# Twelve of 22 feature tiles of each FFN's last projection by a seven-product block scheme, with the accumulators corrected in place in PSUM

## The chip, the cores and the metric

The kernel runs on one core of a Trainium2 chip. The metric is the device time of one execution in microseconds (us); lower is better. A difference of under 0.2%, about 2.2 us here, cannot be told from no change.

## The reference

One layer of an encoder on 512 tokens of width 1024, all in float32: a half-step SwiGLU feed-forward network (FFN), two attention branches that are merged by gates, and a second FFN. The change touches the last matrix product of `_swiglu`, in both FFNs:

```python
D_MODEL, SEQ, D_FF = 1024, 512, 2816

def _swiglu(x, w_gate, w_up, w_down):
    return (jax.nn.silu(x @ w_gate) * (x @ w_up)) @ w_down
...
f = _swiglu(_rmsnorm(x, ffn1_pre_g[l]), ffn1_w_gate[l], ffn1_w_up[l], ffn1_w_down[l])
x = x + 0.5 * _rmsnorm(f, ffn1_post_g[l])
```

With 128 features to a tile, `@ w_down` multiplies 512 tokens by 22 feature tiles by 1024 columns.

## The kernel before

Every float32 product is made of three TensorE matmuls on fp32r halves (`mm3`): high by high, high by low, low by high. `split` makes the halves: ScalarE (ACT) casts the value to the high half, VectorE (DVE) subtracts to get the low half. Weights come in pieces of 128 x 1024 numbers (512 KB): `convert` loads one on SyncE's (SP's) DMA queue into a buffer of tag `raw` (two buffers) and splits it into two buffers of tag `w` (twelve buffers, so six split pieces at a time). Other SBUF tiles of 128 x 512 come from a pool of 54 units; PSUM has eight banks of 128 x 512.

An FFN runs in stages. The normed input is `hn_hi`, `hn_lo`, feature-major (8 feature tiles by 512 tokens). Gate and up products of the first three output tiles are plain (`first_pairs`, `pair`). For the other 19 tile pairs `seven` already uses a block scheme with seven products of 12 matmuls of width 256 instead of eight; sums of weight blocks come from accumulating DMAs on GpSimd's (POOL's) queue (`load_blocks`) and from DVE (`sums_of`). `use` and `use7` apply SiLU and leave each hidden tile in `hidden[j]`.

`token_major` is the last projection (and, with eight tiles, the output projection of the mixing stage). Tokens are stationary, weights move, 512 columns at a time. It sums the left 512 columns of all four token tiles over the 22 feature tiles (`acc0`, four banks), then the right 512 columns over the first 14 (`acc1`), then, token tile by token tile, over the last eight, so that the post-norm of one token tile runs beside the matmuls of the next. Each hidden tile is split once (`stat`). In all 22 x 4 x 2 = 176 `mm3`, 528 matmuls of width 512, in each FFN. While the last tile pairs of `seven` are under way, `behind` already converts pieces for `token_major`.

The order on each engine is made when the program is built, by a list scheduler with priorities in the order of the code; in the stretches of `ordered` (the end of an FFN and the start of the next stage) PE, ACT and DVE keep the order of the code, and SP does through the whole first FFN. Each engine and each DMA queue then runs its list in order.

Of the kernel before, what the change touches and what calls it, by code (L numbers as in the profile page):

```python
# [12 lines left out]
F32 = mybir.dt.float32  # L13
# [3 lines left out]
ALU = mybir.AluOpType  # L17
# [23 lines left out]
def block_kernel(ctx, tc, x, gains, weights, rpb_near, rpb_all, alibi0, alibi12, out):  # L41
    nc = tc.nc

    const = ctx.enter_context(tc.tile_pool(name="const", bufs=1))
    big = ctx.enter_context(tc.tile_pool(name="big", bufs=1))
    wp = ctx.enter_context(tc.tile_pool(name="wp", bufs=2 * NPIECE))
    gp = ctx.enter_context(tc.tile_pool(name="gp", bufs=2))
    up = ctx.enter_context(tc.tile_pool(name="up", bufs=NUNIT))
    sp = ctx.enter_context(tc.tile_pool(name="sp", bufs=4))
    pp = ctx.enter_context(tc.tile_pool(name="pp", bufs=8, space=PSUM))  # L50
    dp = ctx.enter_context(tc.tile_pool(name="dp", bufs=1, space=DRAM))
# [11 lines left out]
    def bank(name="ps"):  # L63
        return pp.tile([P, 512], F32, tag="ps", name=name)

    hn_hi = big.tile([P, NK, T], F32R, name="hn_hi")
    hn_lo = big.tile([P, NK, T], F32R, name="hn_lo")
    ident = const.tile([P, P], F32, name="ident")
    mhalf = const.tile([P, 1], F32, name="mhalf")

# [17 lines left out]

    pieces = {}
    loads = deque()  # L90
    state = {"next": 0, "take": 0, "stop": 2 * STD, "ahead": lambda: None}
    ordered = []
    total = weights.shape[0]

# [130 lines left out]
        late.append(lambda: [turned(t, b, xs[b]) for b in range(2)])  # L225

    def turned(t, b, xs):
        pt = bank()
        for i in range(4):
            nc.tensor.transpose(pt[:, i * P:(i + 1) * P], xs[:, i * P:(i + 1) * P], ident)  # L230
# [62 lines left out]
        split(w[:, :512], w[:, 512:], raw)  # L293
        return w

    def seven(use, mv, n_pairs, n0, behind, raws):

        blocks = {}
        o = {}

        def get(j):
            if j < n_pairs and j not in raws:
                raws[j] = load_blocks(n0 + 2 * j)

        def ready(j, i):
            if j < n_pairs:  # L310
                if j and loads:
                    loads.popleft()()
                if i == 1:
                    sums_of(raws[j])
                blocks[j, i] = split_block(raws[j].pop(i))
            elif behind:
                behind()
# [12 lines left out]
        get(0)  # L330
        get(1)
        for i in (1, 5, 2, 6, 3, 7, 4):
            ready(0, i)
        for j in range(n_pairs + 1):
            now, was = j < n_pairs, j > 0
            get(j + 2)
            if now:
                q = product(j, 1, "q", True)
                g, u = res[j] = unit(name="g"), unit(name="up")
                nc.scalar.copy(g[:, :256], q)  # L340
            ready(j + 1, 1)
            if was:
                q0 = product(j - 1, 7, "q", False)
                g0, u0 = res.pop(j - 1)
                nc.vector.tensor_tensor(u0[:, 256:], u0[:, 256:], q0, op=ALU.subtract)
# [12 lines left out]
            ready(j + 1, 3)  # L358
            if was:
                product(j - 1, 4, "q", False)  # L360
                use(j - 1, g0, u0, q0)
            ready(j + 1, 7)
            if now:
                product(j, 3, "p", False)
                nc.vector.tensor_tensor(u[:, :256], p, u[:, :256], op=ALU.subtract)
            ready(j + 1, 4)

    def token_major(n_k, stat, g_post, f, g_pre, store, src=None):

        wt = {}
        first = max(n_k - 8, 0)
        early = [] if store else [n for n in sorted(spread) if n >= state["next"]][:SPREAD]

        def one(acc, t, k, i, start, stop):
            hh, hl = stat(k)
            if t == 0 and i < n_k:
                stat(min(k + 2, n_k - 1))  # L380
            if i // 2 not in wt:
                wt[i // 2] = take(k < first)
            s = slice(t * P, (t + 1) * P)
            mm3(acc, hh[:, s], hl[:, s], *cut(wt[i // 2], (i % 2) * 512, 512), start, stop)

        acc0 = [bank() for _ in range(NT)]
        for k in range(n_k):
            if first == 0 and k % 2 and early:
                convert(early.pop(0))
            for t in range(NT):  # L390
                one(acc0[t], t, k, k, k == 0, k == n_k - 1)
        ss = [small("ssf", 2) for _ in range(NT)]
        for t in range(NT):
            sumsq(acc0[t], ss[t][:, 0:1], f)
        acc1 = [bank() for _ in range(NT)]
        for k in range(first):
            if k > 2 and k % 2 == 0 and early:
                convert(early.pop(0))
            for t in range(NT):
                one(acc1[t], t, k, n_k + k, k == 0, False)  # L400
        fg0 = []
        for t in range(NT):
            u = unit()
# [5 lines left out]
        fill(NPIECE)  # L409
        ordered.append([mark()])  # L410
        for t in range(NT):
            for k in range(first, n_k):
                one(acc1[t], t, k, n_k + k, k == 0, k == n_k - 1)
                if t and not store and k == first + TURN:
                    if t > 1:
                        late.popleft()()
                    pre_norm(t - 1, g_pre, ssx)
# [24 lines left out]

    def ffn(g, store, src):
        hidden = [None] * NF
        parts = {}
        n0 = state["take"]

        def stat(k):
            if k not in parts:
                parts[k] = unit(F32R), unit(F32R)  # L450
                split(*parts[k], hidden[k])
                hidden[k] = None
            return parts[k]

        def use(j, pg, pu):
            h = unit(name="h")
            nc.scalar.activation(h, pg, AF.Silu)
            nc.vector.tensor_tensor(h, pu, h, op=ALU.mult)
            hidden[j] = h

        def use7(j, g, u, q):
            nc.scalar.activation(g[:, :256], g[:, :256], AF.Silu)
            nc.scalar.activation(g[:, 256:], q, AF.Silu)
            nc.vector.tensor_tensor(g, u, g, op=ALU.mult)
            hidden[STD + j] = g
# [20 lines left out]
        def behind():  # L486
            state["next"] = max(state["next"], after)
            state["take"] = after
            fetch()
# [289 lines left out]
    def mixing(g):  # L779
# [168 lines left out]
        token_major(8, lambda k: merged[k], g_post, 1.0, g_pre, False)  # L948


    whole[:] = [[unit(name="whole") for _ in range(2)] for _ in range(2)]
# [167 lines left out]
    return w.reshape(-1, 2, P, w.shape[1] // 512, 512).transpose(3, 0, 2, 1, 4).reshape(-1, P, PIECE)  # L1119


# [43 lines left out]
```

## Time and profile before

| | us |
|---|---|
| median of 3 runs | 1121.98 (1121.58 to 1122.52) |
| the profiled execution | 1121.61 |
| span of its profile | 1119.8 |
| PE busy in the span | 1111.2 (99%) |
| DVE busy | 726.7 (65%) |
| ACT busy | 587.0 (52%) |
| POOL busy | 99.5 (9%) |

The profile shows one execution. PE is TensorE's matmuls and PEld its loads of the stationary operand, which overlap the matmuls. A matmul's time in the profile is from its start to its modelled end, and neighbours overlap, so the rate of PE is read from the starts of consecutive matmuls. The 1.8 us between the span and the profiled execution's time lie outside the profiled instructions.

### The profile page before, as it was taken

What the parts mean: (1) busy time and instruction counts of PE and PEld (TensorE: products, weight loads), DVE (VectorE), ACT (ScalarE), POOL (GpSimd) and SP (SyncE); (2) the same over time, 40 slices, a digit from 0 to 9 for tenths busy, and PEclk for the clock granted to TensorE, in tenths of its full rate; (3) what the DMA queues carried; (4) which work ended last, traced back from release to release, by engine and by line L of the source; (5) the groups of instructions that cost most, each with busy time, mean ns of one, the idle gap of its engine ahead of it and who ended that gap; (6) DMA issues with size and microseconds to landing.
All of it is one profiled execution on the core that took longest, in us unless ns stands there. A gap on an engine that the chain in (4) does not pass through costs nothing.

```text
span 1119.8 us, 18253 instructions
## 1 busy us (share of the span) xinstructions
PE 1111.2 (99%) x6959; PEld 1004.4 (90%) x6959; DVE 726.7 (65%) x1336; ACT 587.0 (52%) x1188; POOL 99.5 (9%) x156
## 2 busy tenths in 40 slices
PE   9999999999999999999999999999999999999997
PEld 7999999998888988888988888889999999998886
DVE  6887777783245678886467645657877777782313
ACT  6555555572233667767656643245555555571210
POOL 3112111000002000000000000013111111000001
PEclk9999999999999999999999999999999999999999
DMA  5889998443362353422232323356577776543412
GB/s 207 218 185 254 230 234 201 108 119 108 94 192 90 109 166 121 132 76 81 72 100 76 85 85 95 95 170 174 127 182 189 162 185 187 123 133 104 169 48 75
DMA packets 77576, 155.71 MB, mean 139 GB/s; under 512 B 22065, under 2 KB 24625, under 8 KB 77490
## 3 DMA queue, kind: packets, MB, share of 16 engines
q1 hardware_dynamic: 63856, 134.17, 37.8%
q0 software_dynamic: 10944, 19.93, 11.5%
q8 instruction: 54, 0.88, 0.3%
q10 hardware_dynamic: 2690, 0.46, 0.2%
q14 instruction: 32, 0.26, 0.1%
HBM read 149.50 MB, written 7.58 MB: 140 GB/s over the span
## 4 chain that ended last, share of the span: by engine, by line
PE 99%; DVE 0%; POOL 0%; issue 0%; ACT 0%; DVEq 0%; POOLq 0%; ACTq 0%
PE ps L154 20%; PE ps L156 20%; PE ps L155 20%; PE q L154 7%; PE q L155 7%; PE q L156 7%; PE p L155 3%; PE p L154 3%; PE p L156 3%; PE r L154 2%; PE r L155 2%; PE r L156 2%; PE ps L692 1%; PE ps L719 1%; PE ps L230 1%; PE ps L661 1%
## 5 line engine op out<-in xcount | busy, mean ns | idle before, releaser
L86 DVE TENSOR_TENSOR w<-raw,w 128x1024 fp32r<-128x1024 f32 (+1 forms) x200 | 194.7, 978 | 210.0 <-ACT w L85 200.3
L85 ACT CAST w<-raw 128x1024 fp32r<-128x1024 f32 (+1 forms) x200 | 169.7, 854 | 237.1 <-PE ps L155 149.9
L154 PE MATMUL ps<-hn_hi,w 128*128 128x512 f32 (+1 forms) x512 | 181.9, 355 | 0.0
L156 PE MATMUL ps<-hn_hi,w 128*128 128x512 f32 (+1 forms) x512 | 179.4, 350 | 0.0
L155 PE MATMUL ps<-hn_lo,w 128*128 128x512 f32 (+1 forms) x512 | 179.3, 350 | 0.0
L154 PE MATMUL ps<-w,u 128*128 128x512 f32 (+1 forms) x456 | 177.2, 389 | 0.0
L155 PE MATMUL ps<-w,u 128*128 128x512 f32 (+1 forms) x456 | 176.8, 388 | 0.0
L156 PE MATMUL ps<-w,u 128*128 128x512 f32 (+1 forms) x456 | 176.8, 388 | 0.0
L86 DVE TENSOR_TENSOR w<-t,w 128x512 fp32r<-128x512 f32 x152 | 104.1, 687 | 32.1 <-ACT w L85 32.1
L85 ACT CAST w<-t 128x512 fp32r<-128x512 f32 x152 | 93.7, 619 | 41.9 <-ACT w L85 17.8
L156 PEld LDWEIGHTS ps<-hn_hi,w 128*128 128x128 f32 x512 | 96.9, 189 | 12.8
L155 PEld LDWEIGHTS ps<-hn_lo,w 128*128 128x128 f32 x512 | 97.0, 190 | 11.5
L154 PEld LDWEIGHTS ps<-hn_hi,w 128*128 128x128 f32 x512 | 97.0, 189 | 11.5
L156 PEld LDWEIGHTS ps<-w,u 128*128 128x128 f32 x456 | 85.7, 188 | 17.5
L154 PEld LDWEIGHTS ps<-w,u 128*128 128x128 f32 x456 | 85.7, 188 | 17.1
L155 PEld LDWEIGHTS ps<-w,u 128*128 128x128 f32 x456 | 85.7, 188 | 16.9
L154 PE MATMUL q<-hn_hi,w 128*128 128x256 f32 x304 | 86.2, 284 | 0.0
L155 PE MATMUL p<-v,w 128*128 128x256 f32 x304 | 86.1, 283 | 0.0
L155 PE MATMUL q<-hn_lo,w 128*128 128x256 f32 x304 | 86.1, 283 | 0.0
L155 PE MATMUL q<-v,w 128*128 128x256 f32 x304 | 86.1, 283 | 0.0
L156 PE MATMUL q<-v,w 128*128 128x256 f32 x304 | 86.1, 283 | 0.0
L156 PE MATMUL q<-hn_hi,w 128*128 128x256 f32 x304 | 86.1, 283 | 0.0
(163 smaller groups left out, 2302.1 us busy)
## 6 DMA issues: line engine op xcount, KB each, us to landing
raw<-in_weights_dram SPq DMA_DIRECT2D x156, 512.0 KB
t<-in_weights_dram SPq DMA_DIRECT2D x76, 256.0 KB
t<-in_weights_dram POOLq DMA_DIRECT2D x76, 256.0 KB, 5.3
w<-in_weights_dram SPq DMA_DIRECT2D x38, 256.0 KB
x<-in_x_dram SPq DMA_DIRECT2D x16, 256.0 KB
table<-bias_d SPq DMA_DIRECT2D x12, 256.0 KB
gain<-in_gains_dram SPq DMA_DIRECT2D x5, 512.0 KB
table<-in_alibi_dram SPq DMA_DIRECT2D x8, 256.0 KB
```

The lines of the kernel that those rows point to most:

```text
L85: nc.scalar.copy(hi, src)
L86: nc.vector.tensor_tensor(lo, src, hi.bitcast(F32), op=ALU.subtract)
L154: nc.tensor.matmul(o, sh, mh, start=start, stop=False, **kw)
L155: nc.tensor.matmul(o, sh, ml, start=False, stop=False, **kw)
L156: nc.tensor.matmul(o, sl, mh, start=False, stop=stop, **kw)
L230: nc.tensor.transpose(pt[:, i * P:(i + 1) * P], xs[:, i * P:(i + 1) * P], ident)
L661: nc.tensor.matmul(ps[:, o:o + w], q[:, cols], windows(wide, kl, i), start=False, stop=True)
L692: nc.tensor.transpose(ps[:, i * P:(i + 1) * P], s, ident)
L719: nc.tensor.matmul(o, vv[n][:, h], m, start=first, stop=(n == 3 and part == 1), skip_group_check=True)
```

## The change

Twelve of the 22 feature tiles are taken out of the plain sum. They form three block products: each takes two blocks of two feature tiles, two halves of 256 tokens and two halves of 512 columns, and makes seven products of two feature tiles x 256 tokens x 512 columns (12 matmuls each) instead of eight. With BLOCKS = 6 pairs of feature tiles there are 3 x 7 = 21 products per FFN, in the order of `seq`, where `(i, d)` is product i of block product d and `("o", n)` a part of the ten tiles that stay plain. So 12 tiles x 4 x 2 = 96 `mm3` become 84.

The output stands in eight banks: `r` and `c` are the left and right columns of the first 256 tokens, `q` and `z` those of the other 256. Products run into `r`, `q` or `c`; at four places in `seq` (`after`) one accumulator is added to or taken from another by `onto`: ACT copies the two banks to SBUF, DVE adds them to the two others in place, and later matmuls go on summing there.

The token sums are made on DVE (`tokens`) from the hidden tiles, which `times` now writes by half-tokens into `duos`. The weight sums are made by accumulating DMAs of 512 KB on POOL's queue (`t1`, `t3`, `t4`) and by DVE (`t2 = t1 + W11`, under `rows`). Every product needs its own split of a 128 x 512 token tile and of a 128 x 1024 weight tile; `prep` does it six places ahead in `seq` (AHEAD), the first six under the last two rounds of `seven` (`lead`). The 32 KB per partition of `hn_hi`, `hn_lo` become four tiles of a pool `hp`, which the weight sums (`ta`, `tb`, `ba`, `bb`) take over when `seven` has read a half for the last time; `renew` gives them back. The pieces of `w_down` are reordered on the host (`_down_pieces`).

```diff
+BLOCKS = 6
+AHEAD = 6
+ORDER = [*range(STD, STD + 2 * BLOCKS), *range(STD), *range(STD + 2 * BLOCKS, NF)]
-    big = ctx.enter_context(tc.tile_pool(name="big", bufs=1))
+    hp = ctx.enter_context(tc.tile_pool(name="hp", bufs=4))
...
-        seven(use7, next(sums), NF - STD, n0 + 2 * STD, behind, raws)
-        token_major(NF, stat, g_post, 4.0, g_pre, store, src)
+        far, lead, rest = down(after, duos, stat, g_post, g_pre, store, src)
+        state["next"] = state["take"] = after + 2 * BLOCKS
+        seven(use7, next(sums), NF - STD, n0 + 2 * STD, lambda q: [f() for f in q.popleft()], far, lead, raws)
+        rest()
...
+            if kind == "t1":
+                raw[key] = duo_room(*at)
+                nc.sync.dma_start(raw[key], block(0, 0, d))
+                nc.gpsimd.dma_start(raw[key], block(0, 1, d), accum_op=add)
+                return
...
+            if kind == "t3":
+                nc.sync.dma_start(raw[key], block(0, 1, d))
+                nc.gpsimd.dma_start(raw[key], block(1, 1, d), accum_op=add)
...
+        def fourth(d):
+            raw["t4", d] = raw.pop(("t2", d))
+            nc.gpsimd.dma_start(raw["t4", d], block(1, 0, d), accum_op=add)
...
+            x, y, op = {5: (hc, hd, sub), 6: (v[d], ha, sub), 3: (v[d], hb, add)}[i]
+            nc.vector.tensor_tensor(v[d], x, y, op=op)
...
+            if i == 6:
+                t = raw["t2", d] = raw.pop(("t1", d))
+                nc.vector.tensor_tensor(t, t, raw[(1, 1), d], op=add)
+                return t
...
+                split_tokens(s, tokens(*s))
+                split_rows(s, rows(*s))
+        into = {1: "q", 2: "r", 3: "c", 4: "q", 5: "c", 6: "q", 7: "q"}
...
+        def onto(x, y, op):
+            for t in range(2):
+                u = unit(name="part")
+                with tc.high_priority(offset=URGENT):
+                    nc.scalar.copy(u, acc[y][t])
+                nc.vector.tensor_tensor(acc[x][t], acc[x][t], u, op=op)
+        after = {(1, 2): ("r", "q", add), (5, 2): ("z", "c", add), (6, 2): ("c", "q", sub), (7, 2): ("z", "q", sub)}
+        seq = [(2, 0), (2, 1), (1, 0), (1, 1), (1, 2), ("o", 1), (5, 0), (5, 1), (5, 2), (6, 0), ("o", 2),
+               (6, 1), (6, 2), (2, 2), (7, 0), (7, 1), (7, 2), (3, 0), ("o", 3), (3, 1), ("o", 4), (3, 2),
+               ("o", 5), (4, 0), ("o", 6), (4, 1), ("o", 7), (4, 2)]
+        far = deque([[ld(((1, 0), 0), "u"), ld(((1, 0), 1), "u")], [ld(((0, 0), 0)), ld(((0, 0), 1))], []])
+        lead = deque([
+            [ld(("t1", 0), "ta", 0)], [pr(0)], [ld(("t1", 1), "ta", 1)], [pr(1)], [ld(((0, 0), 2))],
+            [pr(2)], [ld(("t1", 2), "tb", 0)], [pr(3)], [], [pr(4)], [], [pr(5)], [], []])
...
```

What it moves on the engines is seen best where the first FFN passes from `seven` to the last projection. DVE before, behind its last correction of a gate/up tile: it splits hidden tiles (`g` to `u`) and pieces (`raw` to `w`).

```order
L86 TENSOR_TENSOR u_3511<-g_1803,u_3510 128x512
L86 TENSOR_TENSOR w_3262<-raw_3259,w_3261 128x1024
L86 TENSOR_TENSOR u_3527<-g_1943,u_3526 128x512
L86 TENSOR_TENSOR u_3543<-g_2083,u_3542 128x512
L86 TENSOR_TENSOR u_3559<-g_2223,u_3558 128x512
```

DVE now, somewhat later, at the splits of products (6, 0) and (6, 1): L610 makes `t2`, L604 token sums, L672 the correction in PSUM, L111 the splits.

```order
L610 TENSOR_TENSOR ta_3198<-ta_3198,ba_3390 128x1024
L111 TENSOR_TENSOR a_3459<-v_3380,a_3458 128x512
L610 TENSOR_TENSOR ta_3198<-ta_3198,ba_3390 128x1024
L604 TENSOR_TENSOR v_3431<-v_3431,h_1488 128x512
L610 TENSOR_TENSOR tb_3315<-tb_3315,bb_3417 128x1024
L672 TENSOR_TENSOR r_3393<-r_3393,part_3495 128x512
L604 TENSOR_TENSOR v_3380<-v_3380,h_1772 128x512
L111 TENSOR_TENSOR w_3464<-ta_3198,w_3463 128x1024
L672 TENSOR_TENSOR r_3394<-r_3394,part_3498 128x512
L111 TENSOR_TENSOR a_3503<-v_3407,a_3502 128x512
L111 TENSOR_TENSOR w_3508<-ta_3198,w_3507 128x1024
```

The split of the weights of (6, 0) now stands behind three sums that need the loads into `ba` and `bb`, and behind a correction that needs product (1, 2).

POOL before, at the end of the first FFN's `seven`: the two accumulating loads of a tile pair (L281, L282), then nothing until the norm.

```order
L281 DMA t1_2757<-in_weights_dram 128x512
L282 DMA t3_2758<-in_weights_dram 128x512
L281 DMA t1_2890<-in_weights_dram 128x512
L282 DMA t3_2891<-in_weights_dram 128x512
L212 TENSOR_SCALAR ms0_4046<-ssf_3710 128x1
```

POOL now: nine accumulating loads of twice the size, for `t1` (L558), `t3` (L568) and `t4` (L574).

```order
L309 DMA t1_2916<-in_weights_dram 128x512
L310 DMA t3_2917<-in_weights_dram 128x512
L558 DMA ta_3198<-in_weights_dram 128x1024 x2
L558 DMA tb_3315<-in_weights_dram 128x1024
L568 DMA tb_3315<-in_weights_dram 128x1024
L568 DMA bb_3417<-in_weights_dram 128x1024
L568 DMA raw_3535<-in_weights_dram 128x1024
L574 DMA ta_3198<-in_weights_dram 128x1024 x2
L574 DMA tb_3315<-in_weights_dram 128x1024
L237 TENSOR_SCALAR ms0_4172<-ssf_3376 128x1
```

A stretch in which POOL's queue was empty now carries nine loads whose data the products wait for.

ACT before, near the end of `seven`: splits alone (and a SiLU, L463).

```order
L463 ACTIVATE g_3157<-q_3144 128x256
L85 CAST u_3606<-g_2643 128x512
L85 CAST u_3622<-g_2778 128x512
L85 CAST u_3638<-g_2911 128x512
L85 CAST u_3654<-g_3034 128x512
L85 CAST w_3286<-raw_3284 128x1024
```

ACT now, where it copies `c` out of PSUM (L671) before the plain part ("o", 2) may go on summing there:

```order
L110 CAST w_3531<-tb_3315 128x1024
L110 CAST w_3556<-raw_3467 128x1024
L110 CAST a_3574<-v_3572 128x512
L110 CAST w_3578<-tb_3315 128x1024
L671 COPY part_3594<-c_3538 128x512
L671 COPY part_3597<-c_3539 128x512
```

The copies stand behind the cast `w_3578`, which reads `t3` of block product 0 and so waits for the fourth accumulating load.

More of the change, by code (lines that the diff above doesn't have):

```diff
@@ L90, in block_kernel @@
     loads = deque()
-    state = {"next": 0, "take": 0, "stop": 2 * STD, "ahead": lambda: None}
+    state = {"used": False, "next": 0, "take": 0, "stop": 2 * STD, "ahead": lambda: None}
     ordered = []
@@ L294, in split_block, with seven @@
         return w
-    def seven(use, mv, n_pairs, n0, behind, raws):
+    def seven(use, mv, n_pairs, n0, behind, far, lead, raws):
         blocks = {}
@@ L307, in get @@
                 raws[j] = load_blocks(n0 + 2 * j)
+            elif j >= n_pairs:
+                behind(far)
         def ready(j, i):
@@ L315, in ready @@
                 blocks[j, i] = split_block(raws[j].pop(i))
-            elif behind:
-                behind()
+            else:
+                behind(lead)
         def product(j, i, key, start):
@@ L411, in token_major @@
         for t in range(NT):
-            for k in range(first, n_k):
-                one(acc1[t], t, k, n_k + k, k == 0, k == n_k - 1)
-                if t and not store and k == first + TURN:
+            for k in ks:
+                one(t, k)
+                if t and not store and k == ks[TURN]:
                     if t > 1:
@@ L444, in ffn, with times @@
         hidden = [None] * NF
+        duos = [[None] * BLOCKS for _ in range(2)]
         parts = {}
         n0 = state["take"]
+        def times(j, a, b):
+            k = ORDER.index(j)
+            if k >= 2 * BLOCKS:
+                hidden[k] = b
+                nc.vector.tensor_tensor(b, a, b, op=ALU.mult)
+                return
+            for i in range(2):
+                if k % 2 == 0:
+                    duos[i][k // 2] = unit(name="h")
+                to = duos[i][k // 2][:, (k % 2) * 256:(k % 2) * 256 + 256]
+                part = slice(i * 256, i * 256 + 256)
+                nc.vector.tensor_tensor(to, a[:, part], b[:, part], op=ALU.mult)
         def stat(k):
@@ L457, in use @@
             nc.scalar.activation(h, pg, AF.Silu)
[L458 to L459 removed]
+            times(j, pu, h)
         def use7(j, g, u, q):
```

203 lines of the change are left out of this document (175 added, 28 removed).

## The prediction

> **What bounds the kernel now.** I read the busy times first, then the chain that ended last, then what PE waited for, and last the last projection of the first FFN by itself. The first fence has one line of the page's busy times and one of its chain, by engine:
>
> ```profile
> PE 1111.2 (99%) x6959; PEld 1004.4 (90%) x6959; DVE 726.7 (65%) x1336; ACT 587.0 (52%) x1188; POOL 99.5 (9%) x156
> PE 99%; DVE 0%; POOL 0%; issue 0%; ACT 0%; DVEq 0%; POOLq 0%; ACTq 0%
> ```
>
> PE fills the span, and the chain that ends last is PE for 99%. All the waits of PE in the trace are two:
>
> ```profile
> PE warm L987 <- DVE idle L955: 1.2, 1, 1.2
> PE ps L230 <- DVE u L1005: 0.6, 1, 0.6
> ```
>
> They come to 1.8 us, at the start. So PE has no stall to lose around the change: each matmul taken out shortens the run by its interval, and each new stall lengthens it by its whole length. The windows by stage (us, then busy time and count of PE, PEld, DVE, ACT, POOL, then granted clock, DMA share, GB/s): `seven`, the last projection of the first FFN, and that of the second:
>
> ```profile
> 128.00:246.00 118.00, 118.00 (x957) 116.75 (x956) 90.53 (x151) 72.81 (x144) 15.91 (x18) 1.00 0.68 176
> 255.00:345.00 90.00, 90.00 (x399) 74.56 (x398) 27.77 (x30) 24.51 (x34) 0.49 (x2) 1.00 0.45 142
> 1010.00:1100.00 90.00, 90.00 (x398) 74.56 (x397) 21.83 (x21) 17.52 (x24) 2.15 (x6) 1.00 0.30 96
> ```
>
> In the last projection DVE is busy for 28 of 90 us and ACT for 25; the spare time there is what the change uses. In `seven`, where the first products are prepared, DVE is already busy for 91 of 118 us.
>
> **What is taken out.** The last projection's matmuls run evenly; of 31 in a row, the first and the last:
>
> ```profile
> 255.00 0.39 PE L156 MATMUL ps<-w,u 128*128 128x512 f32 x1
> 261.80 0.39 PE L156 MATMUL ps<-w,u 128*128 128x512 f32 x1
> ```
>
> 30 intervals in 6.80 us are 0.2267 us each. Per FFN 96 `mm3` become 84, so 36 matmuls go: 8.16 us, and 16.3 us for both. What runs after PE's last matmul stays. The profiled execution took 1121.61 us (span 1119.8 and 1.8 around it), so 1105.3; its time lies 0.4 us under the median of the runs, 1121.98, and from the median the sum is **1105.7 us**. That holds if DVE, ACT and the loads keep ahead.
>
> **What is added on DVE and ACT.** Times by start to next start, from the end of `seven` in the first FFN:
>
> ```profile
> 239.10 0.42 DVE L365 TENSOR_TENSOR up<-p,up 128x256 f32<-128x256 f32 x1
> 239.43 0.68 DVE L464 TENSOR_TENSOR g<-up,g 128x512 f32<-128x512 f32 x1
> 240.03 1.89 DVE L86 TENSOR_TENSOR u<-g,u 128x512 fp32r<-128x512 f32 x3
> 241.84 0.41 DVE L345 TENSOR_TENSOR up<-up,q 128x256 f32<-128x256 f32 x1
> 242.17 3.10 DVE L86 TENSOR_TENSOR u<-g,u 128x512 fp32r<-128x512 f32 x5
> 245.18 1.22 DVE L86 TENSOR_TENSOR w<-raw,w 128x1024 fp32r<-128x1024 f32 x1
> 246.31 1.29 DVE L86 TENSOR_TENSOR u<-g,u 128x512 fp32r<-128x512 f32 x2
> L404 DVE TENSOR_TENSOR u<-ps,gain 128x512 f32<-128x512 f32 x12 | 7.7, 683 | 2.2 <-ACT junk L204 2.1
> L594 ACT COPY vt<-ps 128x512 f32<-128x512 f32 x4 | 2.3, 580 | 0.0
> ```
>
> A 512-wide operation takes 0.60 us (five in 3.01), a 1024-wide one 1.13, a 256-wide one 0.33. Of the last two rows, from the groups, one reads PSUM on DVE at 683 ns, the duration of a read from SBUF, so `onto` gets 0.60; the other is a copy on ACT, 0.58. Per FFN: 21 products split 0.60 + 1.13 = 36.3 us; 12 token sums 7.2; three `t2` 3.4; eight corrections 4.8; together 51.7, in place of twelve hidden tiles and twelve pieces at 20.8. That is 31 us more on DVE, over 110 us in which it had about 75 us free: no cost by its sum. ACT gets nine more splits at 1.67 and eight copies at 0.58, some 20 us in as much room. `times` now writes halves: 12 x (2 x 0.33 - 0.60) = 0.7 us more DVE in `seven`, covered by its 27 us of idle time. What can cost is only order: whether one split is late for its product.
>
> DVE's order from the product of the last gate/up tile (239.43): up to the split of (5, 2) stand four 1024-wide, nine 512-wide and one 256-wide operation, 10.3 us, to 249.7. That split's weight buffers come free when PE has finished product (1, 1). PE's rows give when:
>
> ```profile
> 237.32 0.40 PE L154 MATMUL ps<-w,u 128*128 128x512 f32 x1
> ...
> 238.70 0.28 PE L154 MATMUL q<-v,w 128*128 128x256 f32 x1
> 238.82 0.28 PE L155 MATMUL q<-v,w 128*128 128x256 f32 x1
> ...
> 240.14 0.40 PE L154 MATMUL ps<-w,u 128*128 128x512 f32 x1
> L85 ACT CAST w<-raw 128x1024 fp32r<-128x1024 f32 x108 | 113.5, 1053 | 196.6 <-PE ps L155 149.6 <-DMA raw<-in_weights_dram 32.7 <-issue 5.3
> ```
>
> PE's order has six matmuls, the last but one product of `seven` (12 at 0.12), 26 matmuls (to 246.03), the last product of `seven` (to 247.47), and 16 matmuls: (1, 1) ends at 251.1. ACT's cast takes 1.05, so DVE subtracts at 252.2. From there to the end of the split of (6, 0) are five 1024-wide and five 512-wide operations, 8.7 us: 260.9. PE reaches (6, 0) after 76 matmuls, 247.47 + 17.2 = 264.7. **The slack is 3.8 us** for (6, 0), 4.2 for (6, 1), 3.9 for (6, 2). This is the tightest place I found, and it is why I cost DVE at nothing; by durations in place of intervals 2.9 us are left. If the cover is gone, each us late is a us of the run, and the copies of `c` on ACT are late next.
>
> **What is added on the queues.** Loads grow from 22 to 31 of 512 KB per FFN, nine of them accumulating on POOL's queue. The page's two large queues, the accumulating loads now, their two groups on POOL, one window's answer for tile `t`, and a plain load of 512 KB from its issue to the cast that waited for it:
>
> ```profile
> q1 hardware_dynamic: 63856, 134.17, 37.8%
> q0 software_dynamic: 10944, 19.93, 11.5%
> t<-in_weights_dram POOLq DMA_DIRECT2D x76, 256.0 KB, 5.3
> L282 POOL DMA_DIRECT2D t<-in_weights_dram x38 | 39.5, 1038 | 5.4 <-DMA t<-in_weights_dram 2.0 <-DMA raw<-in_weights_dram 1.2 <-DVE neg L754 0.8
> L281 POOL DMA_DIRECT2D t<-in_weights_dram x38 | 33.2, 874 | 298.3 <-DMA t<-in_weights_dram 108.0 <-DVE w L86 77.2 <-DVE up L345 36.5
> DMA to landing us min/median/max: 3.9/6.3/8.0
> 230.19 0.33 SPq L99 DMA_DIRECT2D raw<-in_weights_dram  x1
> 233.88 1.05 ACT L85 CAST w<-raw 128x1024 fp32r<-128x1024 f32 x1 [0.56 <-DMA raw<-in_weights_dram]
> ```
>
> By volume: q0 took 11.5% of 1119.8 us for 76 loads, 1.7 us each with all sixteen engines, so 3.4 for 512 KB; q1 1.65 for 512 KB. Per FFN nine by 3.4 and no plain load saved (22 remain), 31 us of transfers more against a share of 0.45 in the stage (half of 110 us idle): hidden as a sum. As a latency no row shows an accumulating load of 512 KB. The nearest: two of 256 KB, issued one behind the other, landed by 8.0 us at most; the far end is twice the median in series, 10.6 each. I take 8.0 for the first and 3.4 for each next, since loads sharing engines is what the median of 5.3 for a share of 1.7 looks like, and keep 10.6 in series for the range. POOL's own issue, 0.9 to 1.0 us, has nothing else queued behind it in that stretch.
>
> The first accumulator `t1`(0) needs half of `hn`, read last 72 matmuls of 0.12 before 237.32, so at 228.7; its plain load lands 3.7 us later, 232.4, and POOL issues by 233.4. The load for `t1`(2) lands near 237.5. All three are in by 248.3, where ACT wants `t1`(2) at 251.1. `ba` and `bb` wait for the last product of `seven`, 247.47, and land at 251.1, 252.8 and 254.4; DVE's three sums `t2` stand at 253.9, 255.7 and 257.4. So 2.8 us are spare on each side of the one guess that I could not measure.
>
> SP: loads into `ba`, `bb` wait there for PE until 247.47, and the plain `raw` loads queue behind them; the pieces already converted cover it, since PE needs none of those behind until (2, 2), over 30 us on.
>
> **Rivals.** *Accumulating loads in series (slower).* At 10.6 us each from 233.4, `t1`(2) lands at 265.2, the split of (5, 2) ends at 267.5 in place of 253.3; of the 14.2 late the slack takes 3.8, and 10.4 us per FFN are lost: 1105.7 + 20.8 = 1126.5. It decides from 8.2 us lost per FFN, `t1`(2) landing at about 263, or 9.9 us each. Against it stands the 8.0 for two; for it, that a doubled load may take twice the median, and that POOL's row L281 shows 108 us of waiting for loads of its tile, which are not in the chain only because nothing on PE hung on them.
>
> A stall on PE may cost more than its length. The granted clock after PE's last matmul:
>
> ```profile
> 1112.70 0.39 PE L156 MATMUL ps<-w,u 128*128 128x512 f32 x1
> 1114.00:1116.00 2.00, 0.00 (x0) 0.00 (x0) 1.65 (x4) 0.00 (x0) 0.83 (x2) 1.00 0.00 0
> 1116.00:1118.00 2.00, 0.00 (x0) 0.00 (x0) 0.62 (x2) 0.00 (x0) 0.00 (x0) 0.78 0.78 262
> 1118.00:1119.80 1.80, 0.00 (x0) 0.00 (x0) 0.00 (x0) 0.00 (x0) 0.00 (x0) 0.50 0.00 0
> ```
>
> It stays full for some 4 us and then halves; a stall that long would add to the loss, one of 3 us would not. The Trainium skill, "TensorE: Matmul & The Clock Gate", Part 1 (the HAM clock gate), says that an idle window of about 3.4 us halves the clock until a busy one of about 3.4 us has passed; the trace agrees with the first half. By that rule a stall of 10 us costs an estimated 1.7 us more (3.4 us at half speed), and the series case ends at 1129.9 rather than 1126.5.
>
> *A split late on ACT (gain partly given back).* ACT's copies of `c` out of PSUM stand behind the cast of `w_3578`, which needs `t3`(0), and PE's plain part ("o", 2) may go on in `c` only after them, at 247.47 + 102 matmuls = 270.6. The plain load of `t3`(0) is the next on SP behind `bb` (254.4) and lands at 256.1; its accumulation, issued in 1.0, is in 8.0 later at 265.1, the cast ends at 266.2 and two copies at 267.3: 3.3 us to spare. As the fourth in series (265.2 + 10.6) it would be in at 275.8, the copies would end at 278.0 and each FFN would lose 7.4; half way it is 3.7 each, 7.4 together: **1113.1**. For it: a dozen such in-order meetings, each with only 3 to 4 us to spare. Against: DVE and ACT each have half the stage free to catch up.
>
> *PEld sets the rate.* Then a matmul taken out saves one weight load instead of an interval. In the stage's window 398 loads keep PEld busy for 74.56 us, 0.187 each: 72 x 0.187 = 13.5, and 1108.5. Against it: PEld is 15 of 90 us idle there, while intervals are even. The Trainium skill, "Perfetto Trace Analysis", Identifying the Most-Contended Engine, would judge distance from the limit by weight-load time rather than matmul busy time; here that gives 83% for the stage and does not overturn the even 0.2267.
>
> **How the numbers follow.** The forecast holds at 0.67 (1105.7), a late split 0.18 (1107 to 1118), PEld 0.05, loads in series 0.10 (0.07 slower, 0.03 within what counts as no change: under 0.2%, 2.2 us, nothing can be told). So faster 0.90, same 0.03, slower 0.07. Range: from 1104.3 (the forecast less some 1.4, one and a half times the spread of the three runs) to 1113.1, the middle of the late split; what lies above, some 0.09 of that case and the 0.10, is 0.19.
>
> **What the next profile would show.** Right: 6887 matmuls; PE's waits still about 1.8 us, all at the start; a span near 1103.5; DVE in the first FFN's last projection up from 28 of 90 us to 55 or more. Wrong step by step: PE waiting for ACT at the products (5, 2) to (6, 2) means late loads of `t1`; at ("o", 2), the copies behind `w_3578`; at (6, 0) with DVE as releaser, my ledger; accumulating loads (L558, L568, L574) that take over 9.9 us each, the series. A rate of matmuls other than 0.2267 in the new products would fell the saving itself.

## The result, and the profile after

The changed kernel took 1108.49 us (median of 4 runs, 1108.15 to 1108.89) against 1121.96 us before on the same chip (4 runs, 1121.58 to 1122.52): ratio 0.988, 95% interval 0.9863 to 0.9897. It is faster by 13.5 us where 16.3 were forecast; the time lies in the range, 2.8 us above the forecast. The profiled execution took 1108.66 us with a span of 1106.9. Its busy times and chain:

```profile
PE 1096.3 (99%) x6887; PEld 991.1 (90%) x6887; DVE 791.0 (71%) x1446; ACT 621.7 (56%) x1244; POOL 115.8 (10%) x174
PE 97%; DVE 2%; ACT 0%; issue 0%; POOL 0%; DVEq 0%; POOLq 0%; ACTq 0%
```

The 72 matmuls are gone, and DVE has 2% of the chain that it did not have before. So the first question is whether the matmuls that went were worth their price. The last projection of the second FFN answers it; its first matmul before, and its first and last after (its last before, 1112.70, stands in the prediction):

```profile
990.29 0.40 PE L154 MATMUL ps<-w,u 128*128 128x512 f32 x1
...
984.05 0.40 PE L179 MATMUL r<-w,a 128*128 128x512 f32 x1
1098.29 0.39 PE L181 MATMUL z<-w,u 128*128 128x512 f32 x1
```

From first to last it took 122.41 us and now takes 114.24: 8.17 us less, 36 intervals of 0.227. The saving is there in full. By 984.05 the changed kernel was ahead by 6.24 us, not 8.16: the first FFN lost 1.9. And behind the last matmul the span before went on for 7.1 us (1112.70 to 1119.8), now for 8.6 (1098.29 to 1106.9): 1.5 us more. These three account for it:

| where | us lost |
|---|---|
| first FFN, PE at the end of product (2, 2) | 1.09 |
| first FFN, transposes for the next stage | 0.85 |
| end of the program, behind PE's last matmul | 1.47 |

Their sum is 3.4; 16.3 - 3.4 = 12.9 is the difference of the two spans, 1119.8 - 1106.9. (The medians give 13.5; the first 20 us of a run, before the first FFN's products, differ by up to 1.6 us between the profiled executions of this case.)

Most of the effects below are smaller than the 2.2 us that two times can tell apart, and beside the experiments the kernel before took 1121.52 to 1121.58 us, not 1121.96. So they are read from PE's rows; the times only bear them out. One execution of the first experiment, the profiled one, took 3861.31 us where the other three took 1108.42 to 1109.08, and it is left out.

**The first loss.** All waits of PE in the trace, then PE's, ACT's and DVE's rows around the second of them:

```profile
PE warm L1219 <- DVE idle L1187: 1.2, 1, 1.2
PE r L179 <- ACT w L110: 0.8, 1, 0.8
PE ps L258 <- DVE u L249: 0.4, 1, 0.4
```

```profile
278.08 0.39 PE L181 MATMUL r<-w,a 128*128 128x512 f32 x1
279.26 0.73 PE L179 MATMUL r<-w,u 128*128 128x512 f32 x2 [0.79 <-ACT w L110]
279.83 0.41 PE L179 MATMUL q<-w,a 128*128 128x512 f32 x1
```

```profile
277.12 1.14 ACT L110 CAST a<-v 128x512 fp32r<-128x512 f32 x2 [2.15 <-DVE v L599]
278.17 1.04 ACT L110 CAST w<-raw 128x1024 fp32r<-128x1024 f32 x1
279.11 1.06 ACT L671 COPY part<-q 128x512 f32<-128x512 f32 x2
```

PE waits for the cast of the piece of ("o", 3): the scheduler has put that part's first two matmuls ahead of (7, 0). Behind them (7, 0) goes on in `q`, which ACT must have copied out before (L671). ACT runs its list in order, and cast and copies stand behind a token split (277.12) that waited 2.15 us for a sum of DVE's. The cast has a second late input, the piece itself:

```profile
269.98 1.23 DVE L111 TENSOR_TENSOR w<-raw,w 128x1024 fp32r<-128x1024 f32 x1
271.24 0.33 SPq L124 DMA_DIRECT2D raw<-in_weights_dram  x1
```

Its load was issued at 271.24, when DVE had emptied a `raw` buffer, and the trace has its last packet landing at 277.99, 0.3 us before ACT was through with the token splits. So DVE is late, for both. It has no gap in this stretch; the windows of after, and under the dots the same stretches before:

```profile
232.00:249.00 17.00, 17.00 (x109) 15.45 (x108) 10.98 (x17) 9.14 (x16) 2.62 (x3) 1.00 0.89 212
249.00:258.00 9.00, 9.00 (x42) 7.44 (x41) 9.00 (x13) 4.24 (x8) 0.87 (x1) 1.00 0.97 387
258.00:290.00 32.00, 31.21 (x138) 25.45 (x137) 32.00 (x42) 23.61 (x35) 4.36 (x5) 1.00 0.70 154
255.00:345.00 90.00, 89.22 (x398) 73.56 (x397) 66.14 (x83) 48.17 (x75) 9.49 (x15) 1.00 0.59 167
...
232.00:249.00 17.00, 17.00 (x109) 15.46 (x108) 16.24 (x25) 15.27 (x29) 0.00 (x0) 1.00 0.44 138
258.00:290.00 32.00, 32.00 (x143) 26.52 (x142) 7.00 (x6) 6.07 (x6) 0.00 (x0) 1.00 0.33 99
```

Over the whole stage DVE is busy for 66 of 90 us, but from 249 to 290 us for all of it: it is working off a backlog. And ahead of that, from 232 to 249, it is busy for only 11 of 17 us, while the DMA engines are at 0.89. There it waited (SP's issue, ACT, DVE):

```profile
235.91 0.33 SPq L124 DMA_DIRECT2D raw<-in_weights_dram  x1
...
246.12 1.05 ACT L110 CAST w<-raw 128x1024 fp32r<-128x1024 f32 x1 [7.36 <-DMA raw<-in_weights_dram]
...
240.88 0.42 DVE L375 TENSOR_TENSOR up<-up,q 128x256 f32<-128x256 f32 x1
247.20 1.23 DVE L111 TENSOR_TENSOR w<-raw,w 128x1024 fp32r<-128x1024 f32 x1 [5.90 <-ACT w L110]
```

The piece of ("o", 1) was issued at 235.91 and cast at 246.12, 10.2 us later, where the same load before took 3.7. It shared the engines with two more plain loads and the accumulating loads of `t1`.

The second FFN of the same execution is a control. Its DMA engines are as full at that point, and around the copies PE and ACT have the same order; but DVE has other work ahead of the piece of ("o", 1), and its longest wait there is 1.62 us:

```profile
978.77:995.77 17.00, 17.00 (x109) 15.45 (x108) 14.70 (x22) 10.97 (x20) 3.45 (x4) 1.00 1.02 274
989.11 1.22 DVE L111 TENSOR_TENSOR w<-raw,w 128x1024 fp32r<-128x1024 f32 x1 [1.62 <-ACT w L110]
1022.77 1.05 ACT L110 CAST w<-raw 128x1024 fp32r<-128x1024 f32 x1 [0.57 <-DMA raw<-in_weights_dram]
1023.73 1.06 ACT L671 COPY part<-q 128x512 f32<-128x512 f32 x2
1025.53 0.39 PE L179 MATMUL q<-w,a 128*128 128x512 f32 x1
```

Counted from the first matmul of each last projection (237.28 and 984.05), the copies begin after 41.8 us in the first FFN and after 39.7 in the second, and PE without a stall goes on in `q` after 41.5. In the second FFN it loses nothing. So full engines alone do not make the loss; what differs is how late DVE is.

**The second loss.** Where the first FFN ends, POOL before, and under the dots POOL, DVE and PE after:

```profile
350.11 0.63 POOL L215 TENSOR_SCALAR ms<-ssf,ms 128x1 f32<-128x1 f32 x1 [0.98 <-ACT junk L204]
...
343.01 1.69 POOL L240 TENSOR_SCALAR ms<-ssf,ms 128x1 f32<-128x1 f32 x1 [0.98 <-ACT junk L229]
343.40 1.22 DVE L111 TENSOR_TENSOR w<-raw,w 128x1024 fp32r<-128x1024 f32 x1
350.22 1.32 PE L258 MATMUL ps<-ident,u 128*128 128x128 f32 x8 [0.40 <-DVE u L249]
```

A weight split for the next stage stands on DVE between the norm steps of the first and second token tile; before, it stood ahead of both. POOL's step there took 1.69 us, and 0.63 at its place before, so the norm, and with it PE's transposes, came late. (DVE's own next steps stand behind the split as well; when they were done, DVE waited only 0.17 us more for POOL.) The Trainium skill, "SBUF — State Buffer" (SBUF: two separate sides), says that a DVE operation with two inputs from SBUF and a POOL operation that reads SBUF exclude each other for a whole instruction; the trace agrees, in that POOL's step ends with the 1024-wide subtraction (344.70 and 344.62).

### The profile page after: what moved, and what is told of

It reads as the page before. It is cut to its first block, busy times and chain, and to the rows that moved or that the text cites. A ratio compares the mean times of both kernels' runs of the same rounds, so it can differ in the third digit from the quotient of the medians.

```text
span 1106.9 us, 18356 instructions
## 1 busy us (share of the span) xinstructions
PE 1096.3 (99%) x6887; PEld 991.1 (90%) x6887; DVE 791.0 (71%) x1446; ACT 621.7 (56%) x1244; POOL 115.8 (10%) x174
## 4 chain that ended last, share of the span: by engine, by line
PE 97%; DVE 2%; ACT 0%; issue 0%; POOL 0%; DVEq 0%; POOLq 0%; ACTq 0%
PE ps L179 13%; PE ps L180 13%; PE ps L181 13%; PE q L181 9%; PE q L179 9%; PE q L180 9%; PE p L181 3%; PE p L180 3%; PE p L179 3%; PE r L179 3%; PE r L180 3%; PE r L181 3%; PE c L181 2%; PE c L179 2%; PE c L180 2%; PE ps L924 1%
## 5 line engine op out<-in xcount | busy, mean ns | idle before, releaser
L111 DVE TENSOR_TENSOR w<-raw,w 128x1024 fp32r<-128x1024 f32 (+1 forms) x186 | 177.8, 961 | 135.0 <-ACT w L110 132.7
L110 ACT CAST w<-raw 128x1024 fp32r<-128x1024 f32 (+1 forms) x186 | 155.0, 839 | 167.1 <-PE ps L180 59.7
L179 PE MATMUL ps<-hn,w 128*128 128x512 f32 (+1 forms) x512 | 181.8, 355 | 0.0
L180 PE MATMUL ps<-hn,w 128*128 128x512 f32 (+1 forms) x512 | 179.2, 350 | 0.0
L181 PE MATMUL ps<-hn,w 128*128 128x512 f32 (+1 forms) x512 | 179.1, 350 | 0.0
L111 DVE TENSOR_TENSOR w<-t,w 128x512 fp32r<-128x512 f32 x152 | 104.3, 689 | 31.3 <-ACT w L110 29.6
L181 PEld LDWEIGHTS ps<-hn,w 128*128 128x128 f32 x512 | 96.9, 189 | 12.9
L180 PEld LDWEIGHTS ps<-hn,w 128*128 128x128 f32 x512 | 97.0, 189 | 11.6 <-DVE hn L262 0.2
L179 PEld LDWEIGHTS ps<-hn,w 128*128 128x128 f32 x512 | 97.0, 189 | 11.5
L181 PE MATMUL q<-hn,w 128*128 128x256 f32 x304 | 86.0, 283 | 0.0
L179 PE MATMUL p<-v,w 128*128 128x256 f32 x304 | 86.0, 283 | 0.0
L180 PE MATMUL p<-v,w 128*128 128x256 f32 x304 | 86.0, 283 | 0.0
L180 PE MATMUL q<-v,w 128*128 128x256 f32 x304 | 86.0, 283 | 0.0
L181 PE MATMUL q<-v,w 128*128 128x256 f32 x304 | 86.0, 283 | 0.0
L180 PE MATMUL q<-hn,w 128*128 128x256 f32 x304 | 86.0, 283 | 0.0
L179 PE MATMUL q<-v,w 128*128 128x256 f32 x304 | 86.0, 283 | 0.0
L179 PE MATMUL q<-hn,w 128*128 128x256 f32 x304 | 86.0, 283 | 0.0
L181 PE MATMUL p<-v,w 128*128 128x256 f32 x304 | 85.9, 283 | 0.0
L309 POOL DMA_DIRECT2D t<-in_weights_dram x38 | 33.2, 874 | 296.1 <-DVE w L111 118.5
L179 PEld LDWEIGHTS q<-hn,w 128*128 128x128 f32 x304 | 58.4, 192 | 0.2
L180 PEld LDWEIGHTS q<-hn,w 128*128 128x128 f32 x304 | 58.4, 192 | 0.2
```

Of the source, the lines that this page charges most:

```text
L110: nc.scalar.copy(hi, src)
L111: nc.vector.tensor_tensor(lo, src, hi.bitcast(F32), op=ALU.subtract)
L179: nc.tensor.matmul(o, sh, mh, start=start, stop=False, **kw)
L180: nc.tensor.matmul(o, sh, ml, start=False, stop=False, **kw)
L181: nc.tensor.matmul(o, sl, mh, start=False, stop=stop, **kw)
L309: nc.gpsimd.dma_start(t1, weights[n][:, :512], accum_op=ALU.add)
```

## The experiments

**Each order wrinkle undone by itself.** First, ("o", 3) put back behind (7, 2); nothing else moves:

```diff
+for i in pe[s] if s == ("o", 3) else ():
+    tc.add_manual_dep(i, pe[7, 2][-1].name, ...)
```

> The changed kernel with one thing undone: the first two matmuls of the plain part ("o", 3), which the scheduler had put ahead of the products (7, 0) to (7, 2) of the first FFN, stand behind them; no other engine's order changes. Theory (those two alone were too early for a piece whose split came late): the wait of PE for ACT's cast (0.8 us, 1.05 us of lost intervals) goes and comes back nowhere, PE's last matmul comes 1.05 us earlier, time about 1107.4 us. Rival (DVE's backlog is what counts, and the next product would wait in its place): the stall moves to a product behind, time within 0.3 us of 1108.5.

It took 1109.07 us (1108.42 to 1109.08): no gain. The run with both edits, below, shows PE's row.

Second, one piece less converted ahead at the end of the first FFN:

```diff
-        fill(NPIECE)
+        fill(NPIECE if src is None or store else NPIECE - 1)
```

> The changed kernel with one piece less converted ahead at the end of the first FFN, so that one 128x1024 split (1.13 us on DVE) no longer stands between the steps of the post-norm of the first and the second token tile; PE's order is the same. Theory (that split delays POOL's and DVE's norm steps, and so the transposes for the next stage): the 0.85 us that PE loses at the start of the next stage goes, time about 1107.6 us. Rival (the norm chain is late for another reason, such as the new order of the norm's left columns): the loss stays, time within 0.3 us of 1108.5.

The second loss is gone: two waits of PE are left, and POOL's step takes 0.64 us.

```profile
PE warm L1219 <- DVE idle L1187: 1.2, 1, 1.2
PE r L179 <- ACT w L110: 0.8, 1, 0.8
...
344.06 0.64 POOL L240 TENSOR_SCALAR ms<-ssf,ms 128x1 f32<-128x1 f32 x1 [0.98 <-ACT junk L229]
```

Set against the changed kernel matmul by matmul, this execution was 1.04 us late before the place (it lost 1.0 in the first microseconds) and 0.19 after it: 0.85 gained there. The time, 1108.41 us (1107.66 to 1109.18), does not show it, since the start varies by as much.

Both together:

> The changed kernel with the edits of the first two runs together: ("o", 3) behind (7, 2), and one piece less converted ahead at the end of the first FFN. Theory (two separate order wrinkles): both losses go, 1.05 + 0.85 us, so PE's last matmul comes about 16.3 us earlier than in the kernel before and the time is about 1106.5 us; the span still ends 8.6 us behind PE's last matmul. Rival (DVE's backlog shows at the next product): a wait for ACT or DVE on PE in the first FFN's last projection stays, time about 1107.5 us.

1108.44 us (1108.36 to 1109.48). The 0.85 us came again; the first loss did not go but grew to 1.8, at the next product:

```profile
277.86 0.39 PE L181 MATMUL r<-w,a 128*128 128x512 f32 x1
279.71 0.50 PE L179 MATMUL q<-w,a 128*128 128x512 f32 x1 [1.46 <-ACT part L671]
```

Now it is ACT's copies out of `q` that PE waits for. My theory of two matmuls out of place fell, and the rival held: what is late is late for the product too, and the two early matmuls had filled some of the gap.

**The loads taken away, or made small.** All 18 accumulating loads of the last projections left out, and in another kernel cut to 256 of 1024 columns. In both the scheduler also shifts some steps: the two matmuls of ("o", 3) go back, and on ACT the first copy out of `q` goes ahead of the cast.

> The changed kernel without the 18 accumulating loads of the last projections (the weight sums t1, t3, t4 are left incomplete); all else issues, though the scheduler also shifts some steps. Theory (the loads fill the DMA engines from 232 to 249 us, and the final drain of POOL grows with the accumulating loads of the run): DVE's idle time of 5.9 us at 241 us goes, PE has no stall at ("o", 3), POOL's drain at the end is back at about 4.7 us from 6.2, and the span ends about 7.1 us behind PE's last matmul in place of 8.6; time about 1106.0 us. Rival (the drain is longer for another reason): the end stays 8.6 us behind PE's last matmul, time about 1107.4 us.

> The changed kernel with the same 18 accumulating loads, each of a quarter of the columns (128x256, 128 KB; the weight sums are incomplete). If the final drain of POOL goes by the number of such loads, it stays at about 6.2 us and the time is about 1107.4 us; if by their bytes (9.4 MB more than before fall to 2.4), it is about 5.1 us and the time about 1106.4 us. In both cases DVE's idle time of 5.9 us at 241 us should shrink to below 2 us, since the DMA engines are no longer full there.

Without the loads 1106.13 us (1105.95 to 1107.04), with quarter loads 1107.36 (1107.09 to 1107.62). In neither does PE wait at the products; the second loss stays in both. With quarter loads, the window from 232 to 249 us and DVE's wait in it:

```profile
232.00:249.00 17.00, 17.00 (x109) 15.45 (x108) 14.93 (x22) 10.63 (x18) 2.63 (x3) 1.00 0.51 142
...
243.35 1.23 DVE L111 TENSOR_TENSOR w<-raw,w 128x1024 fp32r<-128x1024 f32 x1 [1.95 <-ACT w L110]
```

The DMA engines are at 0.51 in place of 0.89, DVE idles 1.95 us in place of 5.90, and the first loss is gone. The copies' order did not matter here: with quarter loads the cast and both copies are done at 277.1, and PE goes on in `q` only at 278.33. The end tells the two apart: without the loads the span ends 7.1 us after PE's last matmul, with small ones 8.6, as the theory by number had it.

**The loads made twice as long.** Each of the six loads for `t1` issued twice:

> The changed kernel with each of the six accumulating loads for t1 issued twice (the sums then hold one block twice over), three transfers more per FFN just where the products begin. Theory (loads that share the engines take about 3.7 us each there): t1 of the third block product lands some 11 us later, near 259.5 us, its split is ready near 261.7, 9.5 later than in my ledger; less the slack left (1.0 us measured, 3.8 in the prediction) PE loses 6 to 8.5 us in the first FFN and about as much in the second; time 1120 to 1126 us. Rival (loads are hidden; the waits elsewhere decide): under 2 us lost per FFN, time under 1113.

1126.31 us in its one run, just above what the theory gave. `t1` of the third block product was in at 260.2 us (expected 259.5). PE ended up 6.8 us behind the changed kernel in the first FFN and 10.3 more in the second. PE's largest wait in the first, the rows after it, and the windows around:

```profile
265.23 0.61 PE L179 MATMUL q<-w,a 128*128 128x512 f32 x2
270.14 0.50 PE L180 MATMUL q<-w,a 128*128 128x512 f32 x1 [4.30 <-DVE w L111]
...
271.70 0.63 PE L180 MATMUL q<-w,a 128*128 128x512 f32 x1
...
274.26 0.49 PE L180 MATMUL q<-w,a 128*128 128x512 f32 x1
271.00:275.00 4.00, 4.00 (x12) 3.16 (x11) 4.00 (x6) 1.94 (x3) 1.13 (x2) 0.57 1.04 201
```

So loads that come late can cost the whole gain: with `t1` of the third block product in at 260.2 us, where the changed kernel has it at 248.4, the run is slower than the kernel before. The danger in the prediction's series rival was real. And this stall of 4.5 us cost more than itself: the matmuls from 271.70 to 274.26 stand 0.427 us apart in place of 0.227, at a granted clock of 0.57, some 1.6 us on top. The Trainium skill, "TensorE: Matmul & The Clock Gate", Part 1 (the HAM clock gate), gives about 3.4 us idle as the point and about 3.4 us of half speed, 1.7 us by my estimate in the prediction; the trace agrees. (PE's wait of 3.72 us in this run's second FFN is followed by half speed too; after waits of up to 1.65 us in the other kernels the matmuls soon stand 0.227 us apart again.)

**The end of the program.** In the kernels above the end went with the number of DMAs on POOL's queue (the software DMAs of the expectations; here all of them accumulate). To change that without touching the last projection, `t3` of the block scheme of gate and up is summed by DVE for some tile pairs (in `sums_of`; both addends are in SBUF) in place of an accumulating load:

```diff
-        nc.gpsimd.dma_start(t3, weights[n + 1][:, 512:], accum_op=ALU.add)
+        on_dve or nc.gpsimd.dma_start(t3, weights[n + 1][:, 512:], accum_op=ALU.add)
...
+        on_dve and nc.vector.tensor_tensor(t3, t3, w11, op=ALU.add)
```

Every second pair, on the kernel with both wrinkles undone:

> As the run with both mended, and in the block scheme of the gate and up products t3 is summed by DVE (0.6 us, both addends are in SBUF) for nine tile pairs of each FFN, so that 76 software DMAs run in all, as in the kernel before, though the 18 of the last projection stay. If POOL's final drain goes by the number of software DMAs of the whole run, it is back at 4.74 us and the time is about 1105.1 us; if only the late or large ones count, it stays at 6.2 and the time is about 1106.5. DVE's 5.4 us more per FFN lie beside its 27 us of idle time and should cost nothing.

All pairs:

> As the run with half of t3 on DVE, with all nineteen pairs of each FFN: 56 software DMAs in the run. By 0.082 us each, POOL's drain would take about 3.1 us; the end of the span then waits for SP's output transfers, 5.9 to 6.3 us behind PE's last matmul, in place of POOL's drain, 6.35, so the time gains under 0.5 us against the half version: about 1104.8 us. DVE has 11.4 us more per FFN against 27 us idle. Rival (DVE becomes late in the block scheme): PE waits for DVE there, time over 1106.

They took 1108.64 us (1106.78 to 1111.61) and 1107.48 us (1107.26 to 1107.91), where about 1105.1 and 1104.8 were expected: both missed. POOL's last long DRAIN instruction (two of 0.1 us and less follow) begins 1.6 us after the start of PE's last matmul in every kernel, and the trace has its length:

| kernel | DMAs on POOL | POOL's last DRAIN, us | last matmul's start to end of span, us |
|---|---|---|---|
| before | 76 | 4.74 | 7.1 |
| changed | 94 | 6.21 | 8.6 |
| without the 18 loads | 76 | 4.75 | 7.1 |
| the 18 at a quarter | 94 | 6.21 | 8.6 |
| `t1` twice | 100 | 6.70 | 9.1 |
| half of `t3` on DVE | 76 | 4.75 | 7.1 |
| all of `t3` on DVE | 56 | 5.27 | 7.7 |

From 76 to 100 the DRAIN grows by 0.082 us for each DMA of the whole run, whatever its size and wherever it stands. The three kernels below fit, with 94, 76 and 76 of them and ends of 8.6, 7.1 and 7.1 us. At 56 it should have been 3.1 us and was 5.27: the line does not go on below, and why was not settled. With half of `t3` on DVE the gain at the end came as expected, but PE lost 1.36 us early in the block scheme, near 53 us, where it waited for a cast of ACT's, and the times spread widely. The cause of that is open: with all pairs on DVE, where it has more to do, PE lost nothing there. The first loss, at 2.0 us, stayed there as in the kernel it was built on.

**The cause of the first loss, and a better version.** ACT and DVE wait for the piece of ("o", 1) although the data for (5, 0) are in; so the two change places in `seq`, with one piece less ahead:

```diff
-(1, 2), ("o", 1), (5, 0), (5, 1),
+(1, 2), (5, 0), ("o", 1), (5, 1),
```

> The changed kernel with one piece less converted ahead (as before) and with (5, 0) and ("o", 1) in the other order in the list of steps, so that ACT and DVE prepare (5, 0), whose weight sum lands at 242 us, before the piece of ("o", 1), whose plain load shares the full DMA engines and lands at 246. Theory (DVE's 5.9 us of idle time behind that load is what makes ACT's copies out of q late): DVE idles less than 3 us there, the copies come 2 us or more earlier, and PE's 1.05 us at the end of (2, 2) go; together with the 0.85 at the next stage the time is about 1106.6 us. Rival (ACT's order around the copies makes the loss, not DVE's late start): a stall of about 1 us or more stays in the first FFN's last projection, time 1107.6.

1106.71 us (1106.34 to 1107.9). PE waits only at the start of the run. DVE's wait, and ACT at the copies:

```profile
247.15 0.69 DVE L111 TENSOR_TENSOR a<-v,a 128x512 fp32r<-128x512 f32 x1 [3.28 <-ACT a L110]
...
274.12 1.14 ACT L110 CAST a<-v 128x512 fp32r<-128x512 f32 x2 [0.56 <-DVE v L599]
275.17 0.58 ACT L671 COPY part<-q 128x512 f32<-128x512 f32 x1
277.63 1.05 ACT L110 CAST w<-raw 128x1024 fp32r<-128x1024 f32 x1 [1.88 <-DMA raw<-in_weights_dram]
278.58 0.58 ACT L671 COPY part<-q 128x512 f32<-128x512 f32 x1
```

DVE idles 3.28 us (under 3 was expected), the token split that waited for DVE comes at 274.12 in place of 277.12, and the first copy at 275.17 in place of 279.11. But here the scheduler also moved the first copy ahead of the cast and the early matmuls back, and the rows show that the earlier DVE was not enough by itself: the cast waited for its load until 277.63. Had both copies stood behind it, as in the changed kernel, the first would have begun at 278.58 and ended at 279.16, and PE, which went on in `q` at 277.93, would have lost an estimated 1.3 us. So this run confirms that DVE starts earlier, but it does not decide between the theory and the rival: the swap took away the lateness and changed ACT's order, and what each is worth was not measured.

Last, `t3` on DVE for the last nine tile pairs of each FFN, without and with the swap, both with one piece less ahead:

> The changed kernel with one piece less converted ahead, and with t3 summed by DVE for the last nine tile pairs of each FFN (76 software DMAs in all); PE's order is that of the changed kernel. Software DMAs by their number: POOL's drain 4.75 us. Fewer accumulating loads just ahead of the last projection leave the plain loads more of the DMA engines. PE's 1.05 us in the first FFN: stays by the theory that the load of the ("o", 1) piece beside three accumulating loads makes DVE late (those stay); time 1108.5 - 0.85 - 1.47 = about 1106.2 us. Rival (DVE in the block scheme becomes late, as with every second pair): PE waits there, time over 1107.

> Both of the two runs before together: the steps swapped, one piece less ahead, and t3 by DVE for the last nine tile pairs. Theory: 1.05 + 0.85 + 1.47 us less than the changed kernel, about 1105.1 us, with PE's waits only at the start of the run. If a stall stays in the first FFN, 1106.2.

Without the swap 1106.41 us (1105.37 to 1106.9): the first loss stays (0.8 us of wait, 1.1 in all), the other two are gone. With it **1105.40 us** (1104.97 to 1105.6), ratio to the kernel before 0.9854 (0.9839 to 0.9869): PE's one wait and the span:

```profile
core 0 of [0], span 1103.5 us
...
PE warm L1219 <- DVE idle L1187: 1.2, 1, 1.2
```

That is within 0.3 us of what the prediction gave for a change that loses nothing, 1105.7 us; it took three more changes to the kernel to get there. ACT has the order of the swap here too: its cast waits for its load until 277.13, and the first copy stands ahead of it, at 274.90.

## Why the prediction was right, and where its size was off

The direction, the range and the saving came as forecast. The forecast case, in which nothing is lost on the way, did not: three losses at places to which the sum gave nothing made 3.4 us. The time lies where the late split had been put (1107 to 1118, at 0.18), and the range held it because it reached up to 1113.1 for that case. Of the signs named, 6887 matmuls and a busier DVE (66 of 90 us) came; PE's waits were not all at the start, and none stood at the products that I had listed.

- *What is taken out, 16.3 us:* right. 8.17 us in the second FFN, and the whole of it reached by the last version.
- *"What runs after PE's last matmul stays":* wrong by 1.47 us. POOL's DRAIN at the end is paid by DMAs that I had costed only where they run.
- *Loads, "hidden as a sum":* the step that failed. As a sum they are, at 0.59 of the engines over the stage. But they come in a burst, and I took 3.7 us for a plain load from a time (before, 230.2 to 233.9 us) when the engines stood at 0.54, most of it that load's own; in the burst it took 10.2. The accumulating loads, the guess that I had worried about, landed close to where I had them. The tile views of `t1`'s (the lines of landing take in the tiles' later accumulating loads too):

```profile
L558 POOL DMA_DIRECT2D ta<-in_weights_dram x2: 872/872/872, 232.9 to 234.2; - x2
DMA to landing us min/median/max: 7.8/8.6/11.7
...
L558 POOL DMA_DIRECT2D tb<-in_weights_dram x1: 872/872/872, 242.9 to 242.9; - x1
DMA to landing us min/median/max: 5.5/5.8/8.2
```

  The one issued at 242.9 took 5.5 us: in at 248.4, forecast 248.3. That this one agrees so well is luck: its plain load, which I had in near 237.5, came at 242.4, and its accumulation took less time than I had given it in the queue behind the others; those took 9.3 and 11.7.
- *DVE's ledger, 3.8 us of slack at (6, 0):* mis-sized. Its split ended at 263.6, not 260.9; PE reaches (6, 0) at 264.71, and 1.1 us was left:

```profile
262.37 1.23 DVE L111 TENSOR_TENSOR w<-ta,w 128x1024 fp32r<-128x1024 f32 x1
```

  No row of PE's waits stands at (6, 0); the backlog of 2.7 us broke out at a later meeting, 15 us on.
- *A split late on ACT:* this rival is what happened, in part and at another place: not the copies of `c` before ("o", 2) but those of `q` before (7, 0), and 1.09 us in one FFN where I had priced 3.7 in each.
- *Loads in series:* did not happen, but the run with `t1` doubled shows its price to be real.
- *PEld sets the rate:* its time, 1108.5, is the measured one by chance. The second FFN's 8.17 us are whole intervals, and the last version goes below 1106.
- *The next stage's order* was in no step; 0.85 us. That the scheduler shifts a split of another stage could be read from DVE's order.

## What to carry to other kernels

Latencies read from a trace hold for the load that the DMA engines had there: where a change adds transfers, look at the stretch in which they start, not at the stage's sum, and put its waits into the ledger of every engine that runs in order behind them. A stall that is mended by moving the waiting instruction may reappear at the next one, as it did here; look for what is late ahead of it. And where a change lets a scheduler move other steps too, read their rows before you call the change the cause: the swap made DVE earlier, but ACT's new order was needed as well. After a change to one stage, read the order at its borders and the time behind the last matmul as well.

## What the runs showed of the hardware that I had not expected

POOL's closing DRAIN grows by 0.082 us for each accumulating DMA that POOL's queue issues in the run, between 76 and 100 of them (4.74 to 6.70 us), and not with their size; here that was 1.47 us behind the last matmul, a tenth of the gain. With 56 it was 5.27 us, so it is no plain proportion.
